# A two-layer encoder trunk on one core: the first weight matrix and twenty other weight slabs loaded raw and split on the engines, and silu's table loaded at another place

## The chip, the cores and the metric

The kernel runs on one core of one Trainium2 chip. The core has five engines that run their own instruction queues side by side: TensorE (PE: matmuls, with the weight loads PEld), VectorE (DVE), ScalarE (ACT), GpSimd (POOL) and SyncE (SP). Transfers can be issued from SP's, ACT's and POOL's queues. The metric is the device time of one execution in microseconds (us); smaller is better. The profile is of one execution on the same chip.

## The reference

All tensors are float32. The input x is 512 tokens by 1024. Two layers do, cut to what matters:

```python
for l in range(DEPTH):                                   # 2
    h = rms_norm(x, attn_norm_g[l])
    z = h @ w_in[l]                                      # 1024 x 4352
    qa, ka, va, qb, kb, vb, ga, gb = split(z)            # 512,128,128,512,512,512,1024,1024
    qa, ka = rope(rms_norm(qa)), rope(rms_norm(ka))      # per head of 64
    ya = window_gqa(qa, ka, va, sink_a[l]) @ w_proj_a[l] # 8 heads, 2 for k and v, band of 128
    yb = neighbourhood_attn(rms_norm(qb), rms_norm(kb), vb, rel_bias_b[l]) @ w_proj_b[l]
    mixed = sigmoid(ga) * ya + sigmoid(gb) * yb
    x = x + mixed @ w_out[l]                             # 1024 x 1024
    h = rms_norm(x, ffn_norm_g[l])
    u = silu(h @ w_gate[l]) * (h @ w_up[l])              # 1024 x 2816
    x = x + u @ w_down[l]
```

## The kernel before

**Products in three parts.** TensorE multiplies in a reduced float format. To keep float32's accuracy, each operand is split into a high part (its value rounded to that format) and a low part (the rest), and a product is three matmuls: high by high, low by high, high by low. On activations ACT writes the high part and DVE subtracts it for the low part. For weights the kernel before does it by transfer: `w_load` brings a slab in with a load from POOL's queue that rounds it to the high part; `w_low` has ACT write the negative of the high part, and a second load from POOL's queue adds the raw weights to that. So each such slab crosses from memory twice. The second load needs ACT's pass, and ACT's pass needs the first load.

**Slabs and their order.** The weights are cut into slabs of 512 KB in the order in which TensorE takes them. `slab` notes each slab in `plan` and puts `w_load` and `w_low` on a list of due places: so many us of matmul work before the slab's use (`LEAD_H` 23, `LEAD_L` 15). `tick` counts matmul work and calls what is due, so the engines' instruction order is fixed when the program is built. Between matmuls a planner (`issue`, `Need`, `cost`) takes steps of the attention chains whose operands it reckons ready, by its own table of costs. The feed-forward weights after the leading pairs of columns (class `Quad`) come raw through SP's queue and are split on ACT and DVE; blocks of 512 columns are multiplied by a scheme of seven products of halves instead of eight (`m_step`, in the order 1, 5, 6, 2, 7, 3, 4), where products share sums: product 6 adds to a copy (the seed) that ACT makes of product 1.

**The start.** x comes in eight loads of 128 columns (`x_load`) on SP; the first matrix, w_in's 512 columns for qa, in four slabs, each with two chunks of 128 rows. For each chunk `start` transposes x on TensorE, ACT writes xh (x times the norm's gain, high part), DVE copies x's transposed columns to xT and makes xl, ACT squares xT, and DVE adds the square to a running sum. TensorE does a chunk in four blocks (tokens) of three matmuls; x's next transposes stand behind the first block. After the last chunk the ones product sums the squares over partitions, DVE makes the inverse root (13 small operations), TensorE spreads it (the rstd transposes), and the second matrix, for ka and va, follows. Smaller inputs come on POOL's queue behind the first three slabs: the constants, norm gains, positions (posi), sinks (snk). `chain_tables` makes from them the negated sinks (nsnk) and the sine and cosine tables (trig).

**The output projection and the feed-forward part.** Four times two slabs of w_out; after each pair of columns DVE adds the result to xT and `Norm.chunk` makes xh, xl, squares and sums for the next norm. Then the leading 256 columns of w_gate and of w_up, two slabs each; in between, the ones product and the root as above. silu runs first on the gate pair's results.

All engine calls go through one helper, so the profile shows them under one line, 308.

Of the kernel before, what the change touches and what calls it, by code (L numbers as in the profile page):

```python
# [19 lines left out]
P = 128  # L20
# [193 lines left out]
def trunk(ctx: ExitStack, tc: tile.TileContext, a: dict, out: bass.AP, lay: Layout):  # L214
# [59 lines left out]
    def cost(eng, name, o, aps):  # L274
# [11 lines left out]
        if eng == "dve":  # L286
            fast = name in ("tensor_copy", "tensor_scalar") and not in_psum
            return n * (0.52 if fast else 6.4 if name == "reciprocal" else 1.04) + 0.075
# [141 lines left out]

    def tick(dt):
        pos[0] += dt
        while due and due[0][0] <= pos[0]:
            due.pop(0)[2]()
# [15 lines left out]
    def plan_pair(w, col, parts, row0=0):  # L450
        for k0 in range(0, parts, 4):
            n = min(4, parts - k0)
            r = row0 + P * k0
            slab(n, 256, [(0, w[r : r + P * n, col : col + 256])], 2 * n)
# [28 lines left out]
    def plan_ffn(l):  # L483
        plan_pair(a["w_gate"][l], 0, KD)
# [17 lines left out]
    highs, lows, used = {}, {}, [0]  # L502
# [82 lines left out]
    for l in range(DEPTH):  # L585
# [15 lines left out]
        for c in range(4):  # L601
            plan_pair(a["w_out"][l], 256 * c, KD)
# [34 lines left out]
    warm = cp.tile([P, 2], F32, tag="warm", name="warm")  # L637
    A.copy(warm, ones)
# [30 lines left out]
    GQ.dma_start(snk, a["sink_a"].rearrange("l h -> (l h)").unsqueeze(0).to_broadcast([P, DEPTH * 8]))  # L669
    ps = at_bank()  # L670
# [146 lines left out]
    def token_matmul(nrm, evac, begin=None):  # L817

        ps = [mm_bank() for _ in range(NB)]
        if begin is not None:  # L820
            begin(0, False)
            w_low(0)
            begin(0, True)
            begin(1, False)
            begin(1, True)
            tick(0.0)
        for k0 in range(0, KD, 2):
# [4 lines left out]
            for i, (b, k) in enumerate(order):  # L832
# [9 lines left out]
                if begin is not None and i in (0, 2, 4, 6) and k0 < KD - 2:  # L842
                    begin(k0 + 2 + i // 4, i % 4 == 2)
# [749 lines left out]
```

## Time and profile before

| | |
|---|---|
| median of three runs | 1441.97 us (1440.86 to 1449.07) |
| the profiled execution | 1444.73 us, span 1442.9 us |
| busy, share of the span | PE 97%, weight loads 85%, DVE 63%, ACT 49%, POOL 25% |
| granted TensorE clock | 0.993 of full speed |
| transfers | 221.10 MB, of which POOL's queue 165.13 |
| instructions | 20988 |

The span runs from the first to the last instruction; the profiled execution's own time lies 1.8 us above it. A busy TensorE means here that matmuls follow each other without a pause, so what can be gained lies in the few places where it waits. "arena" is the store from which nearly all buffers are cut; "mm" and "at" are banks of the accumulation memory. A row of the timeline gives the start in us, the duration, engine, line, operation, what it writes and reads with shapes, the count of instructions merged, and in brackets the idle time before it and what ended that.

### The profile page before, as it was taken

Reading aid. Unit: us, or ns where it says so; the run is one execution under the profiler, and the core shown is the slowest. Engines: PE = TensorE matmul, PEld = TensorE weight load, DVE = VectorE, ACT = ScalarE, POOL = GpSimd, SP = SyncE. Lnnn points to the kernel's source line nnn. Section 1 sums busy time; section 2 is a strip of 40 time slices with the busy share of each in tenths; the row PEclk is TensorE's granted clock in tenths of the full one; section 3 lists DMA queues with packets and bytes.
Section 4 is the critical chain, followed back from the end, with each engine's and each line's share of the span. In section 5 each row is a group of like instructions: output and inputs, shape, how many; then the busy total and the mean of one; then the engine's idle time right before and its main releaser. Section 6 shows DMA issues by size and latency. Waiting matters only on the chain.

```text
span 1442.9 us, 20988 instructions
## 1 busy us (share of the span) xinstructions
PE 1394.6 (97%) x8074; PEld 1224.6 (85%) x8074; DVE 912.2 (63%) x1752; ACT 706.8 (49%) x1191; POOL 363.4 (25%) x370
## 2 busy tenths in 40 slices
PE   5999999999989999999999999999998999999998
PEld 3778888888779999999987788888887999999997
DVE  3977777543667565665648768783448666574753
ACT  3476766643454343433544776574346343343431
POOL 4533222233221111101244322223232120111110
PEclk9999999999999999999999999999998999999999
DMA  9977788799865645645699678888996674736555
GB/s 226 170 159 129 140 161 157 142 196 259 146 139 144 156 117 143 155 112 117 134 201 174 132 129 155 160 158 155 260 206 109 147 175 116 178 89 145 121 100 117
DMA packets 209316, 221.10 MB, mean 153 GB/s; under 512 B 25900, under 2 KB 177632, under 8 KB 209216
## 3 DMA queue, kind: packets, MB, share of 16 engines
q0 software_dynamic: 157808, 165.13, 61.3%
q1 hardware_dynamic: 51408, 54.62, 13.3%
q8 instruction: 64, 1.05, 0.3%
q14 instruction: 36, 0.29, 0.1%
HBM read 207.13 MB, written 2.10 MB: 145 GB/s over the span
## 4 chain that ended last, share of the span: by engine, by line
PE 77%; DVE 12%; issue 3%; DMA 3%; ACT 3%; POOL 1%; DVEq 0%; POOLq 0%; ACTq 0%
PE mm L308 60%; PE at L308 18%; DVE arena L308 9%; ACT arena L308 3%; DVE sm L308 3%; DMA arena<-in_w_in 2%; DMA arena<-in_w_up 1%; POOL arena L308 1%; DMA cst<-in_consts 1%; DVE hf L308 0%; DVE den L308 0%; ACT L308 0%; ACT mm L308 0%; ACT sm L308 0%; DVEq L308 0%
## 5 line engine op out<-in xcount | busy, mean ns | idle before, releaser
L308 PE MATMUL mm<-arena 128*128 128x512 f32 (+1 forms) x5568 | 1123.6, 357 | 20.7 <-ACT mm L308 12.5
L308 PEld LDWEIGHTS mm<-arena 128*128 128x128 f32 x5568 | 907.1, 191 | 150.3 <-ACT mm L308 12.9
L308 ACT ACTIVATE arena<-arena 128x1024 fp32r<-128x1024 f32 (+3 forms) x276 | 232.7, 862 | 188.8 <-DMA arena<-in_w_down 58.9
L308 ACT CAST arena<-arena 128x1024 fp32r<-128x1024 f32 (+2 forms) x250 | 212.0, 864 | 220.9 <-DVE arena L308 218.5
L308 PE MATMUL at<-arena 128*128 128x256 f32 (+2 forms) x1952 | 303.8, 296 | 5.0 <-DVE arena L308 3.5
L308 PEld LDWEIGHTS at<-arena 128*128 128x128 f32 x1952 | 265.7, 191 | 25.9 <-DVE arena L308 8.1
L308 DVE TENSOR_TENSOR arena<-arena,arena 128x1024 fp32r<-128x1024 f32 (+2 forms) x240 | 233.0, 984 | 59.7 <-ACT arena L308 59.3
L308 DVE TENSOR_TENSOR arena<-arena,mm 128x512 f32<-128x512 f32 x144 | 98.7, 686 | 248.4 <-PE mm L308 248.3
L308 POOL DMA_DIRECT2D arena<-in_w_in x168 | 168.3, 1368 | 339.3 <-ACT arena L308 329.5
L308 POOL DMA_DIRECT2D arena<-in_w_down x96 | 98.2, 1218 | 502.1 <-ACT arena L308 357.5
L308 DVE TENSOR_TENSOR arena<-arena 128x1024 f32<-128x1024 f32 (+3 forms) x196 | 158.3, 823 | 4.0 <-ACT arena L308 1.5
L308 DVE TENSOR_TENSOR arena<-at,arena 128x384 fp32r<-128x384 f32 (+4 forms) x206 | 114.4, 562 | 49.6 <-ACT arena L308 42.2
L308 ACT CAST arena<-at 128x384 fp32r<-128x384 f32 (+2 forms) x164 | 74.4, 459 | 117.2 <-PE at L308 99.9
L308 PE MATMUL at<-cst,arena 128*128 128x128 f32 x504 | 85.9, 277 | 9.7 <-DVE arena L308 5.7
L308 PEld LDWEIGHTS at<-cst,arena 128*128 128x128 f32 x504 | 64.3, 142 | 26.8 <-DVE arena L308 6.8
L308 ACT ACTIVATE arena<-arena,negm 128x256 f32<-128x256 f32 (+1 forms) x128 | 71.4, 559 | 6.5 <-DVE negm L308 5.7
L308 DVE TENSOR_TENSOR arena<-mm,arena 128x512 f32<-128x512 f32 x72 | 49.3, 686 | 33.7 <-PE mm L308 33.6
L308 ACT COPY arena<-at 64x512 f32<-64x512 f32 (+1 forms) x60 | 34.9, 582 | 69.8 <-PE at L308 68.5
L308 POOL DMA_DIRECT2D arena<-in_w_out x32 | 35.1, 1287 | 60.5 <-ACT arena L308 60.5
L308 DVE CUSTOM_DVE_ANT_0 arena<-at,cst,nsnk 128x256 f32<-128x256 f32 (+1 forms) x64 | 34.4, 546 | 18.0 <-PE at L308 17.7
L308 DVE CUSTOM_DVE_ANT_0 arena<-at,arena 128x256 f32<-128x256 f32 (+1 forms) x64 | 30.7, 484 | 15.0 <-PE at L308 14.6
L308 DVE TENSOR_SCALAR arena<-arena,sm 128x384 f32<-128x384 f32 (+1 forms) x102 | 33.9, 387 | 1.1
(70 smaller groups left out, 436.4 us busy)
## 6 DMA issues: line engine op xcount, KB each, us to landing
arena<-in_w_in POOLq DMA_DIRECT2D x104, 512.0 KB, 7.2
arena<-in_w_down POOLq DMA_DIRECT2D x80, 512.0 KB, 6.7
arena<-in_w_gate SPq DMA_DIRECT2D x20, 1024.0 KB, 7.5
arena<-in_w_up SPq DMA_DIRECT2D x20, 1024.0 KB, 5.3
arena<-in_w_in POOLq DMA_DIRECT2D x64, 256.0 KB, 6.3
arena<-in_w_out POOLq DMA_DIRECT2D x32, 512.0 KB, 8.4
arena<-in_w_proj_a POOLq DMA_DIRECT2D x16, 512.0 KB, 7.0
arena<-in_w_proj_b POOLq DMA_DIRECT2D x16, 512.0 KB, 5.9
```

The costliest lines, as they stand in the source:

```text
L308: f(*args, **kw)
```

## The change

**The first matrix.** Its four slabs are loaded raw: the first, in two halves, from ACT's queue, the others from POOL's at the places where the high parts were loaded. For each chunk ACT copies the high part and DVE subtracts for the low part (`first_parts`, called by `start` ahead of x's transposes). The copy to xT moves from DVE to ACT. `start` is no longer in two halves: a chunk is prepared as a whole, behind the first block of the chunk before it. The norm gains' two loads move from SP's to ACT's queue, the constants' load on SP goes ahead of x's first, and ACT's first use (`warm`) stands behind its loads.

**w_out and the leading pair of w_gate.** Their ten slabs in each layer are loaded raw from SP's queue 23 us of matmul work ahead (`w_raw`), and split 9 us ahead by an ACT copy and a DVE subtraction (`w_parts`).

**silu's table.** A silu of two columns stands behind the last chunk of the output projection, so that the table is loaded there.

**The planner.** DVE's cost of a scalar_tensor_tensor outside the accumulation memory rises from 0.075 to 0.13 us beside its size.

```diff
+LEAD_R, LEAD_P = 23.0, 9.0
-def slab(n, width, src, units, later_h=0.0, later_l=0.0):
+def slab(n, width, src, units, later_h=0.0, later_l=0.0, on_engines=False):
     i = len(plan)
     plan.append((n, width, src))
-    at_pos(total[0] - LEAD_H + later_h, lambda: w_load(i))
-    at_pos(total[0] - LEAD_L + later_l, lambda: w_low(i))
+    if on_engines:
+        at_pos(total[0] - LEAD_R, lambda: w_raw(i))
+        at_pos(total[0] - LEAD_P, lambda: w_parts(i))
+    else:
+        at_pos(total[0] - LEAD_H + later_h, lambda: w_load(i))
+        at_pos(total[0] - LEAD_L + later_l, lambda: w_low(i))
...
-    plan_pair(a["w_gate"][l], 0, KD)
+    plan_pair(a["w_gate"][l], 0, KD, on_engines=True)
...
-        plan_pair(a["w_out"][l], 256 * c, KD)
+        plan_pair(a["w_out"][l], 256 * c, KD, on_engines=True)
...
+def w_raw(i):
+    n1, n2, ((_, ap),) = plan[i]
+    raws[i] = buf([n1, n2])
+    Q.dma_start(raws[i], ap.rearrange("(k p) n -> p k n", p=P))
+def w_parts(i):
+    n1, n2, _ = plan[i]
+    highs[i], lows[i] = buf([n1, n2], F32R), buf([n1, n2], F32R)
+    A.copy(highs[i], raws[i])
+    soon(lambda: V.tensor_tensor(lows[i], raws[i], highs[i].bitcast(F32), ALU.subtract), 1.2)
+def first_load(i):
+    n1, n2, ((_, ap),) = plan[i]
+    raws[i] = buf([n1, n2])
+    ap = ap.rearrange("(k p) n -> p k n", p=P)
+    if i:
+        GQ.dma_start(raws[i], ap)
+    else:
+        for k in range(2):
+            AQ.dma_start(raws[i][:, k], ap[:, k])
+    highs[i], lows[i] = buf([n1, n2], F32R), buf([n1, n2], F32R)
+def first_parts(k):
+    raw, h, lo = raws[k // 2][:, k % 2], highs[k // 2][:, k % 2], lows[k // 2][:, k % 2]
+    A.copy(h, raw)
+    V.tensor_tensor(lo, raw, h.bitcast(F32), ALU.subtract)
...
-    x_load(0)
     Q.dma_start(ident, a["consts"][:, :P])
     for i, n in enumerate(("attn_norm_g", "ffn_norm_g")):
-        Q.dma_start(vec[16 * i : 16 * i + 16], a[n].rearrange("l (k p) -> (l k) p", p=P))
-    w_load(0)
-    for c in range(1, KD):
+        AQ.dma_start(vec[16 * i : 16 * i + 16], a[n].rearrange("l (k p) -> (l k) p", p=P))
+    for c in range(KD):
         x_load(c)
-        if c in (3, 5):
-            w_load((0, 3, 5).index(c))
+        if c % 2 == 0:
+            first_load(c // 2)
...
-            if begin is not None and i in (0, 2, 4, 6) and k0 < KD - 2:
-                begin(k0 + 2 + i // 4, i % 4 == 2)
+            if begin is not None and b == 0 and kk + 1 < KD:
+                begin(kk + 1)
...
-def start(nrm, k, second):
-    if not second:
-        ps = at_bank()
-        for b in range(NB):
-            T.transpose(ps[:, P * b : P * b + P], xin[k][:, b, :], ident)
-        A.activation(held(nrm.xh[k]), by_columns(ps), AF.Copy, scale=gain(0, k))
-        V.tensor_copy(held(xT[k]), by_columns(ps))
-        return
+def start(nrm, k):
+    first_parts(k)
+    ps = at_bank()
+    for b in range(NB):
+        T.transpose(ps[:, P * b : P * b + P], xin[k][:, b, :], ident)
+    A.activation(held(nrm.xh[k]), by_columns(ps), AF.Copy, scale=gain(0, k))
+    A.copy(held(xT[k]), by_columns(ps))
     V.scalar_tensor_tensor(nrm.xl[k], xT[k], gain(0, k), nrm.xh[k].bitcast(F32), ALU.mult, ALU.subtract)
...
     last = l == DEPTH - 1
+    A.activation(warm, ones, AF.Silu)
     spawn(nrm.chain())
```

In the order of the built programs (the helper's line is 308 before, 309 in the change; what an instruction waits for stands in brackets, DMASW being POOL's transfers, DMAHW SP's and ACT's) three places move. First DVE in the first matrix, before: xl and the sum of the fifth chunk, then the negated sinks.

```order
14 L308 SCALAR_TENSOR_TENSOR arena_73<-arena_72,vecT,arena_73 128x512 [waits DVE_49]
15 L308 TENSOR_TENSOR arena_72<-arena_72 128x512 [waits DMAHW6_49,Activation_49]
16 L308 COPY arena_72<-at_223 128x512 [waits Activation_49]
17 L308 CAST vec_76<-posi 4x128 [waits DMASW0_49,Pool_49]
18 L308 TENSOR_SCALAR nsnk<-snk 128x16 [waits DMASW3_49]
19 L308 SCALAR_TENSOR_TENSOR arena_73<-arena_72,vecT,arena_73 128x512 [waits DVE_49]
```

In the change: the low part, xl and the sum of the second chunk, then the negated sinks, then the low part and xl of the third.

```order
4 L309 TENSOR_TENSOR arena_73<-arena_72,arena_73 128x512 [waits DMAHW6_49,Activation_49]
5 L309 SCALAR_TENSOR_TENSOR arena_73<-arena_72,vecT,arena_73 128x512 [waits Activation_49]
6 L309 TENSOR_TENSOR arena_72<-arena_72 128x512 [waits Activation_49]
7 L309 CAST vec_76<-posi 4x128 [waits DMASW0_49,Pool_49]
8 L309 TENSOR_SCALAR nsnk<-snk 128x16 [waits DMASW3_49]
9 L309 TENSOR_TENSOR arena_73<-arena_72,arena_73 128x512 [waits Activation_49]
10 L309 SCALAR_TENSOR_TENSOR arena_73<-arena_72,vecT,arena_73 128x512 [waits Activation_49]
```

The positions' copy and the negated sinks, with their waits for POOL's loads, move from the sixth chunk's place to the third's. Beside it ACT in the first matrix of the change, from the square of the fifth chunk to the copies of the seventh (CAST is the copy to a high part, 128x1024 a pass for the second matrix):

```order
26 L309 ACTIVATE arena_72<-arena_72 128x512 [waits DVE_49,Activation_49]
27 L309 ACT_TABLE_LOAD
28 L309 ACTIVATE trig<-arena_72 128x128 [waits DVE_49]
29 L309 CAST arena_73<-arena_72 128x512
30 L309 ACTIVATE arena_73<-at_264,vecT 128x512 [waits PE_49]
31 L309 COPY arena_72<-at_264 128x512
32 L309 ACTIVATE arena_72<-arena_72 128x512 [waits DMAHW5_49,Activation_49]
33 L309 ACTIVATE arena_73<-arena_73 128x1024 [waits DMASW5_49]
34 L309 ACTIVATE trig<-arena_72 128x128 [waits DVE_49]
35 L309 CAST arena_73<-arena_72 128x512 [waits DMASW2_49]
```

Before, both sine activations and the table's load stood behind the xh of the last chunk. Second, TensorE at the first matrix's end, before:

```order
60 L308 MATMUL at_337<-ones,arena_72 128x1 [waits DVE_49,PE_49,Pool_49]
61 L308 MATMUL at_337<-ones,arena_72 128x1 x3
62 L308 MATMUL mm_121<-arena_73 128x512 x3
63 L308 MATMUL mm_118<-arena_73 128x512 [waits Activation_49]
64 L308 MATMUL mm_118<-arena_73 128x512 x2
65 L308 MATMUL mm_119<-arena_73 128x512 x3
66 L308 MATMUL mm_120<-arena_73 128x512 x3
67 L308 MATMUL mm_121<-arena_73 128x512 x3
68 L308 MATMUL at_389<-cst,rstd_344 128x128 [waits DVE_49]
```

And in the change:

```order
57 L309 MATMUL at_363<-ones,arena_72 128x1 [waits DVE_49,PE_49,Pool_49]
58 L309 MATMUL at_363<-ones,arena_72 128x1 x3
59 L309 MATMUL mm_122<-arena_73 128x512 x3
60 L309 MATMUL mm_123<-arena_73 128x512 x3
61 L309 MATMUL at_402<-cst,rstd_370 128x128 [waits DVE_49,PE_49]
```

Between the ones product and the rstd transposes stand six matmuls instead of 15. Third, DVE at the end of layer 0's output projection, before: the last two additions to xT, and between them the low part of a Quad block.

```order
598 L308 TENSOR_TENSOR arena_72<-arena_72,mm_3213 128x512 [waits PE_49]
599 L308 TENSOR_TENSOR arena_73<-arena_72,arena_73 128x1024 [waits DMAHW7_49,DMASW4_49,Activation_49]
600 L308 TENSOR_TENSOR arena_72<-arena_72,mm_3214 128x512 [waits PE_49]
601 L308 SCALAR_TENSOR_TENSOR arena_73<-arena_72,vecT,arena_73 128x512 [waits Activation_49]
602 L308 TENSOR_TENSOR arena_72<-arena_72 128x512 [waits Activation_49]
```

In the change:

```order
608 L309 TENSOR_TENSOR arena_72<-arena_72,mm_3220 128x512 [waits PE_49]
609 L309 TENSOR_TENSOR arena_73<-arena_72,arena_73 128x1024 [waits DMAHW2_49,Activation_49]
610 L309 TENSOR_TENSOR arena_73<-arena_72,arena_73 128x1024 [waits DMAHW3_49,Activation_49]
611 L309 TENSOR_TENSOR arena_72<-arena_72,mm_3221 128x512 [waits PE_49]
612 L309 SCALAR_TENSOR_TENSOR arena_73<-arena_72,vecT,arena_73 128x512 [waits Activation_49]
```

Two such passes stand there now.

More of the change, by code (lines that the diff above doesn't have):

```diff
@@ L287, in cost @@
             fast = name in ("tensor_copy", "tensor_scalar") and not in_psum
-            return n * (0.52 if fast else 6.4 if name == "reciprocal" else 1.04) + 0.075
+            per = 0.52 if fast else 6.4 if name == "reciprocal" else 1.04
+            return n * per + (0.13 if name == "scalar_tensor_tensor" and not in_psum else 0.075)
         return n * 2.2 + 0.1
@@ L429, in trunk, with soon @@
     seq = []
+    def soon(f, after=0.1):
+        at_pos(pos[0] + after, f)
     def tick(dt):
@@ L669, in trunk @@
     GQ.dma_start(snk, a["sink_a"].rearrange("l h -> (l h)").unsqueeze(0).to_broadcast([P, DEPTH * 8]))
+    warm = cp.tile([P, 2], F32, tag="warm", name="warm")
+    A.copy(warm, ones)
     ps = at_bank()
@@ L1435, in layer @@
         gs = {}
-        def soon(f, after=0.1):
-            at_pos(pos[0] + after, f)
         def quadrant(q, w, i, t, src, sign):
```

15 lines of the change are left out of this document (5 added, 10 removed).

## The prediction

> **What bounds the kernel now.** I read the page first, then whom TensorE waited for, then the timeline at the places where it waited.
>
> ```profile
> span 1442.9 us, 20988 instructions
> ...
> PE mm L308 <- ACT mm L308: 12.5, 2, 6.3
> PE at L308 <- DVE arena L308: 11.5, 15, 2.3
> PE mm L308 <- DMA arena<-in_w_in: 8.3, 1, 8.3
> PE at L308 <- DMA vec<-in_ffn_norm_g: 5.8, 1, 5.8
> PE at L308 <- DMA arena<-in_x: 3.9, 1, 3.9
> ```
>
> The first row is the page's, the others are TensorE's waits (total, times, longest). The five add up to 42 us of 1442.9; nearly all else is matmul. So the change can gain in three places only: the first matrix (8.3, 5.8 and 3.9), one wait in each layer's feed-forward part (two of 6.2, released by an ACT copy), and small waits for DVE. The start, by the timeline (start, duration, instruction; in brackets the idle time before it and what ended it):
>
> ```profile
> 11.01 1.12 PE L308 MATMUL at<-cst,arena 128*128 128x128 f32 x4 [3.89 <-DMA arena<-in_x]
> ...
> 12.02 0.53 POOL L308 DMA_DIRECT2D snk<-in_sink_a  x1 [0.45 <-DMA cst<-in_consts]
> ...
> 20.83 1.22 PE L308 MATMUL mm<-arena 128*128 128x512 f32 x2 [8.28 <-DMA arena<-in_w_in]
> ...
> 26.65 3.00 PE L308 MATMUL mm<-arena 128*128 128x512 f32 x12
> ...
> 29.85 3.01 PE L308 MATMUL mm<-arena 128*128 128x512 f32 x12
> ...
> 35.09 0.17 DVE L308 TENSOR_SCALAR nsnk<-snk 128x16 f32<-128x16 f32 x1
> ...
> 41.51 1.13 DVE L308 TENSOR_SCALAR arena<-arena 128x128 f32<-128x128 f32 x5
> ...
> 42.02 0.31 ACT L308 ACTIVATE trig<-arena 128x128 f32<-128x128 f32 x1
> ...
> 43.82 0.94 DVE L308 SCALAR_TENSOR_TENSOR arena<-arena 128x128 f32<-128x128 f32 x3
> ```
>
> ```profile
> 44.05 1.02 PE L308 MATMUL at<-ones,arena 128*128 128x1 f32 x8
> ...
> 44.94 3.71 PE L308 MATMUL mm<-arena 128*128 128x512 f32 x15
> ...
> 45.88 0.15 DVE L308 TENSOR_SCALAR sm<-at 128x4 f32<-128x4 f32 x1
> ...
> 48.96 0.16 DVE L308 SCALAR_TENSOR_TENSOR rstd<-sm,sm 128x4 f32<-128x4 f32 x1
> ...
> 49.18 0.65 PE L308 MATMUL at<-cst,rstd 128*128 128x128 f32 x4 [0.54 <-DVE rstd L308]
> ...
> 49.59 11.87 PE L308 MATMUL mm<-arena 128*128 128x512 f32 x51
> ```
>
> The second matrix begins at 49.59. Before it the first matmul of the first matrix had to wait for an accumulating load until 20.83; from then on TensorE runs at one chunk of 128 rows of the matrix (12 matmuls and four transposes) in 29.85 - 26.65 = 3.2 us.
>
> **Part 1, the first matrix.** The four accumulating loads go, and with them the wait at 20.83. What is late next? In the changed order each chunk needs ACT's copy to the high part, DVE's subtraction for the low part, and x. Prices, by rows that group equal shapes (count, busy us, mean ns):
>
> ```profile
> L308 ACT CAST arena<-arena 128x512 fp32r<-128x512 f32 x76 | 46.9, 619 | 84.9 <-DVE arena L308 84.8
> L308 DVE TENSOR_TENSOR arena<-arena,arena 128x512 fp32r<-128x512 f32 x76 | 52.1, 688 | 24.1 <-ACT arena L308 23.9
> L308 DVE SCALAR_TENSOR_TENSOR arena<-arena,vecT,arena 128x512 fp32r<-128x512 f32 x32 | 23.9, 747 | 5.2 <-ACT arena L308 4.9
> L308 ACT COPY arena<-at 128x512 f32<-128x512 f32 x28 | 16.2, 579 | 50.1 <-PE at L308 50.1
> L308 ACT ACTIVATE arena<-at,vecT 128x512 fp32r<-128x512 f32 x8 | 5.5, 688 | 19.4 <-PE at L308 19.4
> ```
>
> DVE trades a copy of 0.69 for a subtraction of 0.69 per chunk. ACT gains 0.62 + 0.58 per chunk, 9.6 in all, and loses four passes over slabs; with xh, 0.69, and the square, one more pass of 0.62, it does about 2.5 in 3.2 us, so the sum still fits, but its order matters.
>
> The first new wait is DVE's. Before, the negation of the sinks (nsnk, which needs snk's load) ran at 35.09, when everything had landed. In the changed order it stands ahead of the low part of the third chunk; queued behind it are that subtraction, the third chunk's xl and all later ones, and TensorE waits for those. When does snk land?
>
> ```profile
> DMA packets 6241, 5.52 MB, mean 251 GB/s; under 512 B 474, under 2 KB 4750, under 8 KB 6241
> ...
> snk<-in_sink_a POOLq DMA_DIRECT2D x1, 8.0 KB, 5.0
> ```
>
> These are loads of the first 22 us (KB each, us from issue to landing): issued at 12.02 when the constants had landed, snk took 5.0 and landed at 17.0. In the change it still waits on POOL behind the same loads, three slabs and the constants, while ACT's queue adds 0.52 MB of the first slab to the same period: at 251 GB/s that is 2.1 us if it all goes first, 0 if none does. I take 1.3: snk lands at S = 18.3, between 17.0 and 20.
>
> From S the path is: negation 0.17, subtraction 0.69, xl 0.75, the block's last matmul 0.23, hand-overs 0.1: 20.2. Then TensorE has left nine matmuls of the third chunk (2.0 at 11.87 / 51 = 0.23), five chunks of 3.2, the ones product 0.9 (44.05 to 44.94) and the rstd transposes 0.4 (49.18 to 49.59): 20.2 + 19.3 = 39.5.
>
> To this come new waits inside. The two sine tables (trig) now sit in ACT's queue ahead of the copies for chunks 6 and 7, and each needs a DVE chain. After the xl of the chunk before: sum 0.69, five small operations 1.13 (41.51) or three of 0.94 together (43.82) and one more 0.23, sine 0.31 (42.02), then ACT's copy 0.62, xh 0.69, xT 0.58, DVE's xl 0.75 and a matmul 0.23: 5.0, where TensorE's own work covers 3.3. That is 1.7, twice. A low part for the second matrix, a pass of 1.06 like that at 373.80 below, stands in ACT's queue ahead of chunk 5; I put 0.6 of it on the path. Last, the change leaves six matmuls instead of 15 between the ones product and the rstd transposes: the square-root chain takes 49.1 - 45.9 = 3.2, six cover 1.4, a wait of 1.9 where 0.5 stood. Together 5.9, so the second matrix begins at 45.4 instead of 49.59: **4.2 us gained**; 5.5 with S at 17.0, 2.5 at 20. The second matrix's own loads are ahead of this: they follow snk on POOL and have until 45.
>
> **Part 2, output projection and gate.** Removed: 20 accumulating loads of 0.5 MB and their ACT passes; added: the same number of ACT copies and 20 subtractions on DVE.
>
> ```profile
> L308 DVE TENSOR_TENSOR arena<-arena,arena 128x1024 fp32r<-128x1024 f32 x144 | 174.6, 1220 | 35.6 <-ACT arena L308 35.4
> ...
> 331.00:374.00 43.00, 43.00 (x192) 35.59 (x191) 13.62 (x21) 15.16 (x21) 14.96 (x15) 1.00 1.13 228
> 380.30:411.00 30.70, 25.11 (x138) 21.73 (x138) 27.70 (x45) 18.86 (x21) 6.58 (x6) 0.99 0.52 81
> ```
>
> The stretches give busy us of PE, weight loads, DVE, ACT and POOL. In the output projection (first stretch) ten subtractions, 12.2 us, go to a DVE that is busy 13.6 of 43, beside matmuls that never stop: nothing on the path, but for its seam with the gate, in layer 0:
>
> ```profile
> 373.80 1.06 ACT L308 ACTIVATE arena<-arena 128x1024 fp32r<-128x1024 f32 x1 [4.73 <-DMA arena<-in_w_up]
> ...
> 375.83 1.22 DVE L308 TENSOR_TENSOR arena<-arena,arena 128x1024 fp32r<-128x1024 f32 x1 [3.91 <-ACT arena L308]
> ...
> 376.98 0.68 DVE L308 TENSOR_TENSOR arena<-arena,mm 128x512 f32<-128x512 f32 x1
> ...
> 380.33 1.02 PE L308 MATMUL at<-ones,arena 128*128 128x1 f32 x8 [2.34 <-DVE arena L308]
> ...
> 397.48 1.28 ACT L308 ACT_TABLE_LOAD   x1
> 398.78 1.15 ACT L308 ACTIVATE arena<-arena 128x512 f32<-128x512 f32 x2
> ...
> 401.85 1.22 DVE L308 TENSOR_TENSOR arena<-arena,arena 128x1024 fp32r<-128x1024 f32 x1 [0.87 <-ACT arena L308]
> ...
> 411.61 5.49 PE L308 MATMUL mm<-arena 128*128 128x256 f32 x24 [6.17 <-ACT mm L308]
> ```
>
> ACT waited 4.73 for w_up's load, DVE's subtraction and the last residual addition stood behind it, and TensorE lost 2.3 at the ones product. With DMA relieved (its share there is 1.13, saturated) and POOL without loads that wait for ACT, w_up lands earlier, and I take this wait as gone. But two subtractions (2.44) now stand between the last two residual additions, which are one block of 12 matmuls, 2.7, apart, and the addition ahead takes 0.7: 0.4 late, of which I put 0.2 on the path in each layer. Part 2: 2.3 - 0.4 = **1.9 gained**; 2.3 at best, and at worst a loss of 2.4, if w_up still holds ACT up and one more subtraction of 1.2 comes behind it in each layer.
>
> **Part 3, silu's table.** The load leaves 397.48, where it stood ahead of silu, for the end of the output projection. The wait of 6.2 hangs on DVE, busy 27.7 of 30.7 in the second stretch; the table held it up only through the 0.87 at 401.85. ACT's passes behind it come up to 1.28 earlier, DVE's at most 0.87, and I take 0.7 for each layer: **1.4 gained**, between 0 and 2.6. At its new place the load delays two ACT passes that wait for nothing urgent. At 397.48 the load itself is 1.28 and the next activation starts 0.02 after its end. [...]
>
> **Sum.** 4.2 + 1.9 + 1.4 = 7.5. DVE's changed cost in the planner also reorders the attention stages; the small DVE waits there can go either way, and I take 0, with 2 each way. The profiled execution took 1444.73, 1.8 over its span and 2.8 over the runs' median of 1441.97: it goes to 1437.2, the median to 1434.5.
>
> **Rivals.**
> - *The wait for snk is hidden.* If POOL's loads keep their pace and x's first chunks arrive late themselves, nothing is behind S. x's second chunk, which landed at 11.0, would come at about 10; from there transposes 0.5, nine matmuls 2.1, block 0.7, transposes 0.5, nine 2.1 and a block 0.7 end at 16.5 instead of 20.2: 3.7 more, 1430.8. For it speaks that x was late before too; against it the 5.0 of a load of 8 KB.
> - *The first matrix comes later than before.* Each us of S is one us. From S = 25.8 the 7.5 are gone; with S at 28 the kernel takes 1444.2, slower. It needs the constants on POOL to land 10 us later than before because two other queues share the engines. For it: x's second chunk of 0.26 MB landed only at 11.0. Against it: there is only 0.52 MB more.
> - *The seam stays.* w_up is as late as before, the wait of 2.3 becomes 3.5, and the second layer gets one of 1.2: 1.9 turns into -2.4, 1438.8.
> [...]
> - *The change does not do what it says*: excluded for the loads, whose order shows it; for the table it holds where DVE hides all of it, 1435.9.
>
> **Chances.** My forecast with its own bounds of S 0.58, snk hidden 0.17, the seam stays 0.10, the first matrix later 0.05, the drain 0.03, reordering that outweighs the rest 0.07. The range: S between 17 and 20 gives 1433.2 to 1436.2; with reordering, part 3's bounds and the cases snk hidden (less 2 and 1.2 more of part 3: 1427.6) and the seam (plus 2: 1440.8) it is 1427 to 1442. One per cent, about what a measurement of this kernel can tell, is 14.4 us: faster than 1427.6 needs S hidden and all else at its best, or reordering that helps, 0.16; slower than 1456.4 needs S beyond 40 or a reordering I don't see, 0.05; within, 0.79.
>
> **What would show it.** Right: nsnk on DVE begins at about 18 with a wait for DMA ahead of it, and TensorE's third chunk waits behind it; two waits of 1.7 for ACT before chunks 6 and 7; the first matmul of the second matrix near 45.4; no wait for w_up's load on ACT and under 0.5 us at the ones product of the feed-forward parts; the seed copy's wait at about 5.5 in both layers. Wrong: a first matrix ending before 42 or after 48, a wait for w_out's or w_gate's loads on TensorE, or a total in the attention stages that differs by more than 2 us.

## The result, and the profile after

The changed kernel takes 1428.28 us (median; 1427.95 to 1429.13). The kernel before, over its four runs by then, took 1445.49 (1440.86 to 1449.07). The ratio is 0.9889, with a 95% interval of 0.9867 to 0.9911: 1.1% faster, about 16 us. Those four runs are few and scatter: two lie near 1449 and two near 1441. Beside the experiments below the kernel before ran 7 to 31 times on each of four chips, with medians from 1441.6 to 1443.8. Against these the gain is 13 to 15.5 us. The forecast was 1434.5 with a range of 1427 to 1442. So the direction and the range held, but the gain is about twice the 7.5 that the sum gave. In the profiled executions the span fell from 1442.9 to 1426.4, by 16.5. That of before was itself 2.8 above the median of its first three runs, so up to that much of the 16.5 may belong to this one execution.

The page's head and TensorE's waits of the changed kernel (total, times, longest):

```profile
span 1426.4 us, 20963 instructions
PE 1393.8 (98%) x8074; PEld 1223.7 (86%) x8074; DVE 935.4 (66%) x1768; ACT 713.0 (50%) x1209; POOL 317.7 (22%) x325
```

```profile
PE mm L309 <- ACT mm L309: 10.6, 2, 5.3
PE at L309 <- DVE arena L309: 5.9, 10, 1.5
PE at L309 <- DMA vec<-in_ffn_norm_g: 4.3, 1, 4.3
PE mm L309 <- ACT arena L309: 2.9, 2, 2.4
PE mm L309 <- DVE arena L309: 1.7, 4, 0.8
PE at L309 <- DVE rstd L309: 1.7, 1, 1.7
```

Gone are 8.3 for the first matrix's accumulating load and 3.9 for x. New are ACT and DVE in the first matrix (2.9 and 1.7), and the wait for rstd is 1.7 where it was 0.5. Waits for DVE elsewhere fell from 11.5 to 5.9, and only 2.3 of that is the seam.

Both kernels run the same 5568 projection matmuls in the same order. So the start of the same matmul in both traces says how far the change is ahead at that point. That gives the gain by stage, in us, between these two executions. The last two columns are from experiments told below: the part alone on the kernel before, and what its stage loses when it is taken out of the changed kernel.

| stage | forecast | after against before | part alone | part taken out |
|---|---|---|---|---|
| up to the second matrix | 4.2 | 6.3 | 6.7 | not run |
| attention, layer 0 and 1 | 0 | 2.0 + 2.7 | 2.4 + 2.9 | 1.6 + 2.8 |
| output projection to gate (seam), layer 0 and 1 | 1.9 | 2.6 + 0.2 | 2.6 + 0.2 | 0.5 + 0 |
| seed copy's wait, layer 0 and 1 | 1.4 | 0.9 + 1.0 | 0.9 + (2.3) | 0.9 + 0.9 |
| 48 matmuls behind the seed copy, layer 0 and 1 | 0 | 0.8 + 0.3 | | |
| sum | 7.5 | 16.7 | | |

The 2.3 in brackets contains time given back for an earlier wait. Every row is larger than forecast, and the largest difference is in the attention stages, which the forecast put at nothing.

The first matrix by the timeline of the changed kernel:

```profile
18.23 0.17 DVE L309 TENSOR_SCALAR nsnk<-snk 128x16 f32<-128x16 f32 x1 [3.99 <-DMA snk<-in_sink_a]
18.32 0.68 DVE L309 TENSOR_TENSOR arena<-arena,arena 128x512 fp32r<-128x512 f32 x1
...
19.72 0.50 PE L309 MATMUL mm<-arena 128*128 128x512 f32 x1 [0.17 <-DVE arena L309]
...
23.17 0.74 DVE L309 TENSOR_SCALAR arena<-arena 128x128 f32<-128x128 f32 x3
23.95 0.95 DVE L309 SCALAR_TENSOR_TENSOR arena<-arena 128x128 f32<-128x128 f32 x3
...
26.68 1.14 DVE L309 TENSOR_SCALAR arena<-arena 128x128 f32<-128x128 f32 x5
...
27.19 0.31 ACT L309 ACTIVATE trig<-arena 128x128 f32<-128x128 f32 x1 [0.17 <-DVE arena L309]
...
29.91 0.50 PE L309 MATMUL mm<-arena 128*128 128x512 f32 x1 [0.24 <-DVE arena L309]
...
30.38 0.94 DVE L309 SCALAR_TENSOR_TENSOR arena<-arena 128x128 f32<-128x128 f32 x3
31.35 0.50 DVE L309 TENSOR_SCALAR arena<-arena 128x128 f32<-128x128 f32 x1
...
31.89 0.31 ACT L309 ACTIVATE trig<-arena 128x128 f32<-128x128 f32 x1 [1.20 <-DVE arena L309]
...
33.35 0.79 PE L309 MATMUL mm<-arena 128*128 128x512 f32 x2 [0.43 <-ACT arena L309]
...
34.61 0.50 PE L309 MATMUL mm<-arena 128*128 128x512 f32 x1 [0.47 <-DVE arena L309]
...
42.94 0.62 PE L309 MATMUL at<-cst,rstd 128*128 128x128 f32 x4 [1.66 <-DVE rstd L309]
43.32 0.94 PE L309 MATMUL mm<-arena 128*128 128x512 f32 x3
```

DVE stands 3.99 idle for snk and TensorE's third chunk stands behind it, as said. The two sine tables delay chunks 6 and 7, the first one hardly, and the second matrix begins at 43.32.

The seam of layer 0 in the changed kernel:

```profile
363.59 2.35 DVE L309 TENSOR_TENSOR arena<-arena,arena 128x1024 fp32r<-128x1024 f32 x2
365.86 0.68 DVE L309 TENSOR_TENSOR arena<-arena,mm 128x512 f32<-128x512 f32 x1
...
369.59 0.95 PE L309 MATMUL at<-ones,arena 128*128 128x1 f32 x8
```

The two subtractions do stand between the last residual additions, and the ones product does not wait.

### The profile page after: what moved, and what is told of

The parts are those of the page before. It is cut to its first block, busy times and chain, and to the rows that moved or that the text cites. A ratio compares the mean times of both kernels' runs of the same rounds, so it can differ in the third digit from the quotient of the medians.

```text
span 1426.4 us, 20963 instructions
## 1 busy us (share of the span) xinstructions
PE 1393.8 (98%) x8074; PEld 1223.7 (86%) x8074; DVE 935.4 (66%) x1768; ACT 713.0 (50%) x1209; POOL 317.7 (22%) x325
## 4 chain that ended last, share of the span: by engine, by line
PE 85%; DVE 10%; ACT 2%; DMA 1%; issue 1%; POOL 0%; DVEq 0%; ACTq 0%; POOLq 0%
PE mm L309 65%; PE at L309 20%; DVE arena L309 7%; DVE sm L309 3%; ACT arena L309 2%; DMA cst<-in_consts 1%; DMA snk<-in_sink_a 0%; DMA arena<-in_w_in 0%; POOL arena L309 0%; ACT L309 0%; DVE hf L309 0%; ACT mm L309 0%; DVE den L309 0%; ACT sm L309 0%; DVEq L1619 0%
## 5 line engine op out<-in xcount | busy, mean ns | idle before, releaser
L309 ACT CAST arena<-arena 128x1024 fp32r<-128x1024 f32 (+2 forms) x278 | 236.0, 870 | 235.9 <-DVE arena L309 232.6
L309 DVE TENSOR_TENSOR arena<-arena,arena 128x1024 fp32r<-128x1024 f32 (+2 forms) x268 | 262.2, 993 | 55.5 <-ACT arena L309 55.2
L309 ACT ACTIVATE arena<-arena 128x1024 fp32r<-128x1024 f32 (+3 forms) x252 | 207.6, 843 | 122.4 <-DMA arena<-in_w_down 59.0
L309 POOL DMA_DIRECT2D arena<-in_w_in x163 | 163.1, 1397 | 335.4 <-ACT arena L309 330.6
L309 DVE TENSOR_TENSOR arena<-arena 128x1024 f32<-128x1024 f32 (+4 forms) x196 | 158.5, 823 | 2.5
L309 ACT COPY arena<-at 128x512 f32<-128x512 f32 (+1 forms) x68 | 39.5, 582 | 64.0 <-PE at L309 63.6
L309 ACT ACTIVATE arena<-arena,vecT 128x512 fp32r<-128x512 f32 x24 | 17.4, 726 | 54.4 <-DVE arena L309 53.9
L309 POOL DMA_DIRECT2D arena<-in_w_up x8 | 8.2, 1029 | 125.3 <-PE mm L309 77.7
```

The lines of the kernel that those rows point to most:

```text
L309: f(*args, **kw)
```

## The experiments

### Each part alone

Four kernels take one part each into the kernel before. Times are medians; spans, stages and waits are those of one profiled execution. By the medians, against 1442.32 for the kernel before in 31 runs beside them, the four gain 5.9, 1.8, 2.1 and 5.9; by the spans it is 9.7, 3.6, 1.6 and 7.7. So a difference between two spans is good to some 4 us only, and what follows rests on waits at known places. The first matrix:

```diff
-            begin(0, False)
-            w_low(0)
...
+            begin(0)
```

> The kernel before with the first matrix's part of the change alone: raw slabs, parts made on the engines, the loads and tables in the changed order; output projection, gate, silu's table and the planner's cost as before. Theory A (the terms add up, each part earns what was gained in its own stage of the changed kernel): the second matrix begins at 43.3 as in the changed kernel (49.59 before), 6.3 us earlier, the attention parts keep their pace, and the span is 1442.9 - 6.3 = 1436.6. Rival B (the first matrix shifts the loads of what follows, and the attention parts gain by that): 2 us and more on top between 45 and 375, span 1434.6 or less. By the prediction's term it would be 4.2: 1438.7.

The time was 1436.47, ratio 0.9953 (0.9937 to 0.9968), span 1433.2. The second matrix begins at 42.94, so the stage earns 6.7 by itself and attention only 0.5 more: rival B falls. The remaining 3 us of the span were not expected, and the medians don't have them. The seam wait of layer 0 is gone, though nothing there was changed, and one stands in layer 1 instead. ACT's and TensorE's timeline there, and the stretch behind the wait (start, end and length; busy us of PE, weight loads, DVE, ACT, POOL; clock; DMA share; GB/s):

```profile
1067.08 1.06 ACT L308 ACTIVATE arena<-arena 128x1024 fp32r<-128x1024 f32 x1 [3.87 <-DMA arena<-in_w_up]
...
1073.61 1.02 PE L308 MATMUL at<-ones,arena 128*128 128x1 f32 x8 [0.94 <-DVE arena L308]
```

```profile
1075.40:1078.70 3.30, 3.30 (x10) 2.56 (x9) 2.92 (x13) 1.41 (x2) 0.86 (x1) 0.50 0.98 149
```

Between the first two rows lies the same chain as in layer 0 of the kernel before: w_up's load, ACT's pass, DVE's subtraction, the last residual addition. Layer 1 loses 2.5 by it, 0.9 in the wait and 1.6 in matmuls at a granted clock of 0.50 behind it, and gains 2.1 back at the seed copy.

The output projection and the gate pair:

```diff
-            plan_pair(a["w_out"][l], 256 * c, KD)
+            plan_pair(a["w_out"][l], 256 * c, KD, on_engines=True)
...
-        plan_pair(a["w_gate"][l], 0, KD)
+        plan_pair(a["w_gate"][l], 0, KD, on_engines=True)
```

> The kernel before with the output projection and the leading gate pair raw, their parts made on ACT and DVE; all else as before. Theory A: the wait of 2.3 at the ones product of layer 0's feed-forward part goes, layer 1 gains 0.2, and of the 1.7 and 1.3 gained at the seed copies a part of up to 0.5 each is due to these slabs, the rest to silu's table: span 1440.1, down to 1439.1. Prediction's term: 1.9, 1441.0. Rival (the seam stays, w_up as late as before): 1442.9 or more. The attention parts have the same order on TensorE and should not change by more than 0.3.

The time was 1440.54, ratio 0.9980 (0.9962 to 0.9997), span 1439.3. The seam gains 2.6 and 0.2, and the seed copies gain nothing (less than 0.1), so what was gained there is not due to these slabs. The rest of the 3.6 lies in the start (0.5) and in layer 0's attention (0.5). w_up's first load now lands at 355.5, where it landed at 373.7.

Silu's table:

```diff
         last = l == DEPTH - 1
+        A.activation(warm, ones, AF.Silu)
```

> The kernel before with silu's table loaded at the end of the output projection by one small activation, nothing else. Theory A: it earns the whole 1.28 of the load in each layer, 2.6, and the seed copies' wait of 6.2 becomes about 5.0 to 5.3: span 1440.3. The prediction's term: 0.7 in each layer, since the chain is held by DVE: 1441.5. Rival (DVE hides all of it): 1442.9. [...]

The time was 1440.22, ratio 0.9981 (0.9963 to 0.9999), span 1441.3. In layer 0 the seed copy gains 0.9. Layer 1 can't be read by itself: the seam costs 3.2 there, 1.6 in a wait and 1.6 in the matmuls behind it, of which 2.3 came back at the seed copy.

The planner's price:

```diff
-            return n * (0.52 if fast else 6.4 if name == "reciprocal" else 1.04) + 0.075
+            per = 0.52 if fast else 6.4 if name == "reciprocal" else 1.04
+            return n * per + (0.13 if name == "scalar_tensor_tensor" and not in_psum else 0.075)
```

> The kernel before with the planner's price for DVE's scalar_tensor_tensor at n*1.04 + 0.13 instead of 0.075, nothing else. TensorE's order in the attention parts is then that of the changed kernel. Theory A (the order of the attention parts alone earns the 4.6 us that the changed kernel gained there): layer 0 gains 2.0 and layer 1 2.6 between the second matrix and the last projection, span 1438.3. Rival B (the attention parts gained from the DMA traffic that went, not from the order): 1442.9 within 1. Rival C (the order alone is worse): 1444 or more.

The time was 1436.39, ratio 0.9952 (0.9937 to 0.9968), span 1435.2. Attention gains 2.4 and 2.9, more than in the changed kernel: theory A stands. TensorE's waits in the two attention stretches, first before, then here, then in the kernel of the next part that has everything but this price:

```profile
PE at L308 <- DVE arena L308: 3.4, 6, 0.9
...
PE at L308 <- DVE arena L308: 4.3, 7, 1.0
PE at L308 <- ACT arena L308: 0.6, 1, 0.6
```

```profile
PE at L309 <- DVE arena L309: 2.0, 5, 0.7
PE at L309 <- ACT arena L309: 0.4, 1, 0.4
...
PE at L309 <- DVE arena L309: 2.2, 5, 0.6
```

```profile
PE at L308 <- DVE arena L308: 3.6, 5, 1.2
...
PE at L308 <- DVE arena L308: 4.5, 8, 1.0
```

With the new price the waits for DVE in these stretches fall from 7.7 to 4.2, and with the old one they are 8.1. These waits are 3.5 of the 5.3 gained; the rest was not divided further. One place in the kernel before, where a product came up 0.94 ahead of its operand:

```profile
190.22 0.76 DVE L308 SCALAR_TENSOR_TENSOR arena<-at,gb,arena 64x512 fp32r<-64x512 f32 x1 [0.75 <-ACT arena L308]
...
191.03 0.62 PE L308 MATMUL at<-arena 128*128 128x384 f32 x2 [0.94 <-DVE arena L308]
```

This wait is in neither kernel with the new price. The operation it waits for reads the accumulation memory, so its own price was not raised; it comes at another time because the order ahead of it is another. How the 0.055 more for other operations leads to just this order was not traced further. The seam wait of layer 0 went here too, 2.6, although w_up and all transfers are as before.

### Each part taken out

> The changed kernel with the planner's old price for scalar_tensor_tensor (n*1.04 + 0.075). Theory A (the order of the attention parts is worth 4.6 to 5.2 by itself): those parts fall back, 2.0 to 2.4 in layer 0 and 2.7 to 2.9 in layer 1, the waits of 1.1 ahead of a 384 wide product near 183 and 885 come back, span 1426.4 + 4.9 = 1431.3. Rival (in the company of the other parts the order no longer matters): 1426.4 within 1. The first matrix, the seams and the seed copies stay as in the changed kernel.

The planner's old price in the changed kernel: 1432.85, ratio 0.9938 (0.9923 to 0.9953), span 1430.9. Attention loses 1.6 and 2.8, 4.4 in all, and the waits return (third fence above). Part alone and part taken out agree, so this part earns 4.4 to 5.2 us.

> The changed kernel with the output projection and the leading gate pair loaded by accumulating transfers again, all else changed. Theory A (the wait ahead of the ones product hangs on how long w_up's first load happens to take behind the other transfers, 7.6 to 10.1 us so far, and strikes in one layer or none): a wait of 0 to 2.7 in one of the layers, a third of it won back at the seed copy behind, span 1426.4 to 1428.6. Rival, the prediction's reading (the slabs earn 2.3 in layer 0 and cost 0.2 in each): 1428.3, the wait in layer 0. If neither layer waits, the slabs were worth nothing in this company.

Both `on_engines=True` taken out of the changed kernel: 1428.2, ratio 0.9903 (0.9888 to 0.9918), span 1426.3, the changed kernel's own 1426.4. At layer 0's seam 0.5 is lost, by a wait of 0.30:

```profile
370.01 1.02 PE L309 MATMUL at<-ones,arena 128*128 128x1 f32 x8 [0.30 <-DVE arena L309]
```

So in this company the slabs are worth nothing that the span shows. With accumulating transfers w_up's first load took 7.3 to 10.1 us from issue to landing in the kernels here. Whether the seam waits hangs on that and on where the load falls between others, and it may strike layer 0, layer 1 or neither. The raw slabs take that chance away; in this profile it would have cost 0.5.

> The changed kernel without the small silu activation that loads the table ahead. Theory A (the chain at the seed copy is held by DVE for 0.4 of the load's 1.28, as in the run with the table alone): the waits go from 5.3 to 6.2 in both layers, 0.9 each, span 1428.2. The prediction's 0.7: 1427.8. Rival (the whole load is on the path): 1.28 each, 1429.0. [...]

The small activation taken out of the changed kernel: 1430.79, ratio 0.9921 (0.9907 to 0.9936), span 1430.3. ACT's timeline ahead of the seed copy of layer 0:

```profile
387.59 1.28 ACT L309 ACT_TABLE_LOAD   x1
388.89 1.15 ACT L309 ACTIVATE arena<-arena 128x512 f32<-128x512 f32 x2
```

The seed copy comes 0.88 and 0.87 later, theory A's value in both layers. The load's row has 1.28, with the next activation 0.02 behind its end. The span lost more, 3.9: 0.9 in the first matrix, whose first slab landed later in this execution, and 1.1 and 0.3 in the matmuls behind the seed copies. The matmuls there are the same, but in layer 0 24 of them start 0.22 apart on the mean (401.71 to 407.00), where in the changed kernel 15 did so (the section on the clock).

### What the sinks cost

The negation moves from ahead of the third chunk's low part to the end of the chain of tables. TensorE's and ACT's order stays.

```diff
-        V.tensor_scalar(nsnk, snk, -1.0, None, ALU.mult)
         yield Need("pe", [vec2], [at_slots])
...
+        V.tensor_scalar(nsnk, snk, -1.0, None, ALU.mult)
         done.add("trig")
```

> The changed kernel with the negation of the sinks at the end of the chain of tables instead of ahead of the third chunk's low part on DVE; TensorE's and ACT's order is the same. Theory A (TensorE's waits at the third chunk, 0.83 and 0.17 by the row and 1.4 with the gaps, are all that snk costs, since the chunks behind are late by x anyway): the third chunk's block ends at about 18.6 instead of 19.95, the second matrix begins at 42.0 instead of 43.3, span 1425.1. Rival, the prediction's price (3.7 us): second matrix at 39.6, 1422.7. Rival (the waits of the sine tables take it over): 1426.4, second matrix at 43.3.

The time was 1426.75, ratio 0.9888 (0.9872 to 0.9905), span 1425.5. DVE and TensorE at the third chunk:

```profile
15.43 0.69 DVE L309 TENSOR_TENSOR arena<-arena,arena 128x512 fp32r<-128x512 f32 x1
```

```profile
16.92 2.34 PE L309 MATMUL mm<-arena 128*128 128x512 f32 x9
```

The low part is made at 15.43 instead of 18.32 and the nine matmuls run without a wait. The first matmul came 1.5 later in this execution than in the changed kernel's (9.65 against 8.12), and the second matrix still begins 1.0 earlier, at 42.35. The next chunks do not wait for what was freed: the waits at the sine tables are the same 0.4, 0.6 and 0.7. So snk costs 1.0 at least. The 3.7 of the prediction's rival is not reached: that rival had the third chunk end at 16.5, and here, without any wait for snk, its last nine matmuls begin at 16.92. The first two chunks end later than it assumed; in the changed kernel the matmuls there start 0.43 apart up to 14.25 (last section), where the rival counts 0.23.

### A better kernel

> The changed kernel with two edits: the negation of the sinks at the end of the chain of tables, and in layer 0 the rstd transposes allowed six matmuls later, behind the first six of the second matrix, instead of ahead of it. Theory A: the first edit earns 1.0 to 2.5 (the run with it alone began its first matmul 1.5 later and still gained 1.0 by the second matrix), the second 1.4 of the wait of 1.66 at the transposes; span 1422.5 to 1424.0. Rival (the wait for rstd only moves to the evacuation of the second matrix): 1425.4 to 1424.

```diff
-        yield f"rows{nrm.i}"
...
-        yield from pair_matmul(KD, nrm.xh, nrm.xl, kv_evac)
+        for i, u in enumerate(pair_matmul(KD, nrm.xh, nrm.xl, kv_evac)):
+            if i == (1 if l == 0 else 0):
+                yield f"rows{nrm.i}"
+            yield u
```

The time was 1425.1, ratio 0.9860 (0.9831 to 0.9889), span 1423.8. The wait for rstd falls from 1.7 to 0.3:

```profile
PE at L309 <- DVE rstd L309: 0.3, 1, 0.3
```

At the end of layer 0's attention the kernel is 3.3 ahead of the changed one, where the sinks alone gave 1.3. So the two add up; 1.4 of the 2.0 on top is the wait for rstd, and the other 0.6 lies in smaller waits for DVE in the attention.

> The changed kernel with the split of gate times up (two ACT casts and two DVE subtractions in each layer) issued 6 us of TensorE's work later, so that the seed copy no longer stands behind these casts in ACT's queue. Theory A (the seed copy's wait of 5.3 is a matter of ACT's order: the casts ahead of it wait for DVE, while its own input is there 5 us before): the waits fall to 1.5 or less, and TensorE, which ran 2.8 to 6 us at a granted clock of 0.50 behind each wait, stays at 1.00, which is worth 0.094 for each of the 15 and 24 slow matmuls: 1426.4 - 2 x 4.2 - 3.7 = 1414.3. Rival B (DVE's own chain is as late as the casts, as the prediction read it): 1425.5 or more. Rival C (the waits fall and the clock still halves): 1418.

```diff
-            split(gt[j], h, lo)
+            soon(lambda: split(gt[j], h, lo), 6.0)
```

The time was 1426.55, ratio 0.9871 (0.9847 to 0.9896), span 1425.1. The waits fall from 5.3 to 3.6, not to 1.5. Of the 1.75 gained at each seed copy, 1.0 is lost again at once in layer 0, where 26 instead of 15 matmuls behind it run slowly (granted clock 0.51 from 398.0 to 403.9), and 1.2 in layer 1. There the matmuls behind the seed copy go on at the full rate (a granted clock of 1.00 from 1095.1 to 1101.0), but reach a wait of 1.9 for DVE 48 matmuls later, and from 1101.0 to 1106.8, with that wait in it, the granted clock is 0.72. ACT ahead of the seed copy of layer 0:

```profile
395.39 1.97 ACT L309 CAST arena<-arena 128x1024 fp32r<-128x1024 f32 x2
397.39 0.57 ACT L309 COPY mm<-at 128x512 f32<-128x512 f32 x1
```

Other casts, of the parts that the next products read, are now ahead of the copy, and DVE is busy without a pause from 379 to 397. So both readings have a part: the order in ACT's queue was 1.7 of the 5.3, and most of the rest is put down to DVE's backlog, as the prediction read it; no run took that backlog away.

> All three edits together: sinks' negation later, rstd transposes later in layer 0, split of gate times up later. If they add up as theory A of each has it: 1422.5 to 1424.0 less 12.1, 1410.4 to 1411.9. If the seed copy is held by DVE: 1422 to 1424. If the reordering moves other waits: above 1412 by what the seed copies then wait.

All three edits: 1422.12, ratio 0.9842 (0.9817 to 0.9867), span 1421.2. The gains of the two kernels on the span would add up to 1422.5; the hoped 1411 fails with theory A of the seed copy.

### The clock behind the seed copy

> The kernel with all three edits, and 28 matmuls of 256 columns into a spare bank that nobody reads, in front of the seed copy's first reader in each layer, so that TensorE is busy for 3.4 of the 3.7 us that it waits there; the order of all other instructions is the same. Theory A (TensorE's clock falls to 0.50 because it was idle, and comes back only at the next step of a grid of 3.41 us): the clock stays at 1.00, the 26 and 23 slow matmuls of that kernel run at 0.12 instead of 0.214, 2.4 and 2.2 us less: 1421.2 - 4.6 = 1416.6. Rival B (the low clock has to do with the kind of work behind the wait): 1421.2, or up to 0.3 more. Rival C (DVE's next results are late anyway, so that matmuls at full speed only wait for them): between the two.

```diff
             xh, xl = xs[m]
+            if m == 6 and q == 0 and w == "w_gate":
+                then, spare = clock["pe"], at_bank()
+                h5, x5 = quads[l, q, w].parts[5][0], xs[5][0]
+                for i in range(28):
+                    mm(spare[:, :256], h5[:, i % 4, :P], x5[:, i % 4], True, True)
+                clock["pe"] = then
```

The time was 1421.97 (1420.01 to 1424.81), ratio 0.9869 (0.9846 to 0.9892), no different from the kernel without the 28 matmuls. The span was 1418.2, of an execution of 1420.01; the kernel without them was profiled in one of 1423.02, so the 3.0 between the spans is no result. The granted clock behind the seed copies, by stretches as above, before, after, and in this kernel:

```profile
411.60:416.90 5.30, 5.29 (x24) 5.29 (x25) 0.28 (x1) 2.87 (x4) 3.20 (x3) 0.50 1.10 261
416.90:422.50 5.60, 5.60 (x48) 5.60 (x48) 2.96 (x3) 1.54 (x2) 0.00 (x0) 0.99 1.24 226
```

```profile
399.90:403.30 3.40, 3.39 (x16) 3.39 (x17) 0.28 (x1) 2.87 (x4) 2.17 (x3) 0.50 1.19 241
403.30:407.00 3.70, 3.70 (x32) 3.70 (x32) 2.32 (x3) 0.00 (x0) 1.10 (x2) 0.99 1.18 165
1097.70:1103.10 5.40, 5.40 (x25) 5.40 (x26) 0.22 (x1) 2.82 (x4) 3.23 (x3) 0.50 1.20 224
```

```profile
393.30:396.40 3.10, 3.10 (x26) 3.10 (x27) 2.20 (x3) 1.96 (x3) 1.89 (x3) 1.00 1.09 156
1089.70:1095.00 5.30, 5.26 (x44) 5.26 (x45) 3.60 (x4) 2.80 (x4) 3.22 (x3) 1.00 1.08 155
```

In the first two kernels the matmuls behind the wait run at half the clock, 0.214 apart instead of 0.12; with TensorE kept busy they run at 1.00 from the first. Theory A's cause is shown: the clock fell because TensorE was idle. Its grid of 3.41 us is an estimate (last section). But only 0.5 and 0.15 of the 4.6 arrive behind the seed copies, by rival C. TensorE's waits and its timeline:

```profile
PE mm L309 <- DVE mm L309: 3.8, 2, 1.9
```

```profile
401.19 9.08 PE L309 MATMUL mm<-arena 128*128 128x256 f32 x68 [1.88 <-DVE mm L309]
```

The products behind the next 48 matmuls wait 1.9 in each layer for a sum that DVE writes into their bank. TensorE gets there earlier; DVE doesn't.

## Why the prediction was right or wrong

**What bounds the kernel** held: the gain came from the waits named, the first matrix, the feed-forward parts and the small waits for DVE, but for 1.1 that lies in the clock behind them. That the range held is luck in part. Its lower end, 1427, was drawn for snk hidden and the table at its best, and neither came about; S at 17 and the 2 allowed for reordering give 1431.2.

**Snk and the third chunk: right.** S was put at 18.3 and snk landed at 18.21. The block was to end at 20.2; its last matmul starts at 19.72, and the transposes behind it at 20.06.

**The waits inside the first matrix: too dear.** "That is 1.7, twice" was 0.4 for the first table and 1.3 for the second (the gaps between matmuls, less 0.23 for one). The chain was right for the second: from the end of chunk 6's xl at 29.86 to the waiting matmul at 34.61, with 0.23 for that one, it takes 5.0. For the first it counted five small operations on DVE, 1.13, where the sine stands behind two of them: it begins at 27.19, 0.5 after the five begin at 26.68. The other three belong to the second table. That chain, from 26.16 to 29.91 and 0.23, is 4.0 long. The "0.6 of it on the path" for a low part ahead of chunk 5 was nothing. The rstd wait was 1.8 where 1.9 was forecast. These mis-sized waits, and 0.25 at the third chunk, are 2.6; TensorE's own work came out 0.5 longer than the 19.3. That makes the stage 6.3 instead of 4.2.

**The seam: the wait went, for a reason that holds but wasn't needed.** w_up landed earlier and the 2.3 went, and the 0.2 in each layer for the two subtractions did not appear. But the step treated the wait as a property of the kernel before, that only the slabs could remove. The price alone, the first matrix alone and the table alone each moved or removed it, and without the slabs the changed kernel is no slower. Of the five executions profiled with accumulating slabs only that of before has a long wait in layer 0; two have one in layer 1. One profile's wait for one landing is one draw, and the 2.6 that the table above books here may belong to the execution rather than to the kernel. With one profiled execution of each kernel that stays open.

**The table: right in mechanism, 0.9 for each layer instead of 0.7.** The bound of 0.87 from the row at 401.85 was the value itself. No run shows the drain that has a chance of 0.03: the load's row is 1.28, the next activation starts 0.02 behind it, and 0.9 is earned in each layer.

**Attention: the step that failed.** "I take 0, with 2 each way" set a price of nothing on a change of the order that two experiments put at 4.4 to 5.2. The rows that bound it were in the trace of before: six and seven waits for DVE, 7.7 us in all, in just the stretches that this price orders. That was the upper end of a gain, and 2 was set instead without a row.

**What no step priced: the clock behind a long wait.** 0.8 and 0.3 of the gain lie in matmuls that run at half clock behind the seed copy, and did so for less time in the changed kernel's profile. How long such a stretch lasts did not follow from the wait ahead of it (last section). In the changed kernel, in that with the sinks later and in that with sinks and transposes later, whose seed copies wait equally long, 15, 19 and 17 matmuls were slow in layer 0. So this 1.1 is for the most part luck.

Together: 2.1 for the first matrix, 0.9 for the seam, 0.5 for the table, 4.6 for the order and 1.1 for the clock are the 9.2 between 7.5 and 16.7. The chance of 0.16 for a time under 1427.6 was low for that reason: reordering was priced as a risk, hardly as a gain, and 1428.28 missed that line by 0.7 only.

## What to carry to other kernels

A change to a planner's prices is a change to every stage that it orders: take the sum of the waits in those stages for the engine that is priced anew as what it can earn. Before a wait for one transfer's landing is booked as some edit's gain, ask whether any shift of a microsecond would remove it too; taking the part out of the finished kernel answers that, and adding it alone does not. And a wait of TensorE can cost more than its length (in the kernel with the first matrix alone a wait of 0.9 cost 2.5), so that shortening it by a part may earn less than the part (1.0 of 1.75 was lost again behind layer 0's earlier seed copy).

## What the runs showed of the hardware that was not expected

Behind every seed copy's wait of 4.3 to 6.6 us between two matmuls, and behind three of the four of 3.8, TensorE ran at half its rate for 3.0 to 6.1 us, with a granted clock of 0.50 where the fences above show it. Behind the fourth of 3.8 (layer 1 of the kernel with the later split) it went on at the full rate, 28 matmuls in 3.36 us. The same was seen behind a shorter wait: after the seam wait of 0.94 in layer 1 of the kernel with the first matrix alone the clock was 0.50 over the 3.30 us of its row, and after the 2.34 of the kernel before it was 1.00 (380.3 to 385.0).

How long TensorE ran slowly did not follow from the length of the wait. In the changed kernel both seed copies wait 5.29, and 15 matmuls were slow in one layer and 24 in the other. In the profiles of before and after the granted clock fell to 0.50 within these waits, 2.2 to 5.0 us behind the start of the last matmul. It stayed there for 10.24 us in layer 1 of before and for 6.83 in the other three, 3.41 less. Between the two returns to the full rate of one execution lie 703.28 us before (416.90 and 1120.18) and 699.87 after (403.28 and 1103.15), 3.41 apart too. From these two differences it is an estimate, no more, that the clock changes at points 3.41 us apart, whenever the wait begins. With the earlier seed copy TensorE began 1.9 sooner in layer 0 (398.01 against 399.91) and yet ran slowly until about 403.9, where the changed kernel was back at 403.28: so 1.0 was lost again. In the kernel that was kept busy the clock stayed at 1.00 (third fence of the section on the clock).

TensorE ran at half its rate at the start too, where the profile's clock column shows 1.00. The same twelve matmuls of the second chunk in the changed kernel and in the last experiment, whose instructions are the same there:

```profile
10.69 4.67 PE L309 MATMUL mm<-arena 128*128 128x512 f32 x12
```

```profile
10.68 3.34 PE L309 MATMUL mm<-arena 128*128 128x512 f32 x12
```

They started 0.01 apart in time and took 1.33 more in one than in the other: their starts are 0.43 apart up to 14.25 in the first, and 0.23 from 11.54 on in the second. So a difference of a microsecond in the first matrix of two executions is no result by itself.
